# One encoder block on one core: high-part and low-part matmuls in turn, with the low part 64 bytes further on

## The chip, the cores and the metric

The kernel runs on one core of one Trainium2 chip. The metric is device time in microseconds (us) for one execution. Every weight and activation is float32. A product in full float32 precision is put together from float32r products: each operand is split into a high part (the value rounded to float32r) and a low part (the remainder), and high x high, high x low and low x high are added up.

## The reference

One layer of an encoder on 256 tokens of width 2048, cut here to what the change touches and what stands around it:

```python
h = _rmsnorm(x, norm1_g)
proj = h @ w_in                       # q, k, v and u: 1536 + 512 + 512 + 512 columns
a = _rmsnorm(_window_attention(q, k, v, sink), attn_out_g)
f = _rmsnorm(_fourier_mix(u, w_fourier), fourier_out_g)
x = x + jnp.concatenate([a, f], axis=-1) @ w_out
up = _rmsnorm(x, norm2_g) @ w_up      # gate and value: 2 x 5504 columns
gate = depthwise_conv(up[..., :D_FF], dw_w) + dw_b
x = x + (gelu(gate) * up[..., D_FF:]) @ w_down
return _rmsnorm(x, normf_g)
```

## The kernel before, in words

The work is cut into units of one weight tile each, 128 partitions x 2048 float32 (1 MB). SP loads a tile into one of three `raw` buffers (`load`, L145). `split` (L158) then makes the two parts: ScalarE rounds the tile into a `hi` tile (L165), VectorE subtracts that from the tile and writes a `lo` tile (L166). There are three `hi` and three `lo` buffers. `split` for unit n + 2 is issued behind the matmuls of unit n (`step`, L327; `ff_step`, L967), so the parts are made while earlier units multiply. ScalarE, VectorE, GpSimd and SP each work through their own list in the order written in the program; no scheduler moves anything.

Two kinds of units matter here.

- *Moving weights* (`moving_weights`, L293; `by_parts`, L1041): a 128 x 128 block of the activation is loaded into TensorE as the stationary operand, and 512 columns of weights stream past it. These are the u and v columns of `w_in`, `w_out`, and the down-projection, which for most of its rows is written as products P1, N3, N4, N5, P2, P6, P7. Each stationary block is loaded for a single matmul.
- *Still weights* (`still_weights`, L305): a 128 x 128 block of weights is loaded as the stationary operand and the activation streams past it. These are q and k (16 units) and gate and value (86 units): 102 units. One unit is 16 blocks k. For the high part of block k all 512 columns of `hk(k)` stream, that is the activation's own high part (columns 0 to 255) and low part (256 to 511). For the low part of block k only the 256 columns of the activation's high part stream. So a unit is 16 matmuls of 512 columns (L315, "hi") and 16 of 256 columns (L315, "lo"), all into one PSUM bank, whose two halves are added up later (L827 to L830).

The order within a still-weights unit, before: first the high parts, except for the last `rest` of them, then all 16 low parts, then the `rest` high parts. `rest` is 0, 1 or 2; for q and k it comes from the list `QK_REST` (L53), for gate and value from a rule that counts the high parts between two runs of low parts modulo 3 (L1108 to L1111). The first two gate and value units are interleaved, 12 blocks each and then 4 blocks each (L1114 to L1125).

Before each matmul TensorE loads that matmul's stationary block. This load runs beside the matmul ahead of it, so while one matmul streams its activation, the next matmul's weights are read from SBUF.

Where the tiles lie is fixed by the program. The activation `hT` (and `hU`, which takes its place for gate and value) starts at byte 34,912 of each partition, which is 96 modulo 128; all its blocks are 2048 bytes apart. The `hi` and `lo` buffers start at bytes 92,960 and 119,072 and are 8704 bytes apart, all 32 modulo 128; a tile may begin `SHIFT` = 16 elements (64 bytes) into its buffer (L151 to L156, with a pair of offsets for each unit in `shifts`, L126 and L135). Before, the u and v units have both parts 64 bytes on (96 modulo 128) and all others have none. If addresses are put into two halves by whether they lie in the first or the second 64 bytes of each 128, then for u and v, for `w_out` (whose activation tiles `cat` lie at 32 modulo 128) and for the products (whose operands `op_...` lie at 32 modulo 128), what streams and what is loaded begin in the same half. In the still-weights units before they begin in opposite halves, for the high and the low parts alike. In the attention scores (L619) the 256 columns that stream and the blocks that are loaded are in the same half.

After the first gate and value tiles, the feed-forward part runs gate and value units in a fixed order (`ff_items`, L70): 16 of them at the start, then units and products in turn (four rounds of `PATTERN`, L67, with 56 products in all), then the rest. The last part of the kernel is four tiles of the down-projection, the final norm and the stores.

Of the kernel before, what the change touches and what calls it, by code (L numbers as in the profile page):

```python
# [13 lines left out]
P = 128  # L14
D = 2048
S = 256
NK = D // P
# [13 lines left out]

U_HEAD, U_ROW = 16, 768

SHIFT = 16

V_G2, V_GA, V_GF, V_DW, V_DB, V_SINK = 0, 16, 28, 32, 161, 204
# [12 lines left out]
QK_ORDER = []  # L49
for _g in range(NKV):  # L50
    QK_ORDER += [("k", _g)] + [("q", _g * GQA + _i) for _i in range(GQA)]

QK_REST = [2, 2, 2, 2, 1, 1, 2, 0, 0, 0, 1, 0, 0, 0, 1, 0]  # L53
N_U, N_V, N_QK = 0, 4, 8
N_OUT = N_QK + len(QK_ORDER)

# [13 lines left out]
def ff_items():  # L70


    def ups(tiles):
        return [(kind, j) for j in tiles for kind in ("gate", "val")]

    items = ups(range(8))
    for g in range(N_GROUPS):
        todo = {
            "u": ups(range(8 * g + 8, 8 * g + 16)),
            "s": [("product", g, c, p) for c in range(2) for p in PRODUCTS[c]],  # L80
        }
        items += [todo[c].pop(0) for c in PATTERN]
        assert not any(todo.values())
    items += [("down", 0, c) for c in range(4)] + ups(LAST)
    items += [("down", 1, c) for c in range(4)] + [("last", c) for c in range(4)]
    return items
# [3 lines left out]
def block_kernel(  # L90
# [18 lines left out]
    nc = tc.nc  # L109
# [10 lines left out]
    def bank(pool, name):  # L120
        return pool.tile([P, 512], F32, tag=pool.name, name=name)
# [1 line left out]

    units = [(w_u_x[i], 2048) for i in range(4)] + [(w_in[i], 2048) for i in range(20)]
    units += [(w_out[i], 2048) for i in range(16)]
    shifts = [(SHIFT, SHIFT)] * 8 + [(0, 0)] * 32  # L126
    n_front = len(units)
    items, up_index = ff_items(), {}
    for n, it in enumerate(items):
        if it[0] == "product":  # L130
            continue
        up_index[n] = len(units)
        if it[0] in ("gate", "val"):
            units.append((w_up[2 * it[1] + (it[0] == "val")], 2048))
            shifts.append((0, 0))  # L135
            continue
        elif it[0] == "down":
            units.append((w_down_late[4 * it[1] + it[2]], 2048))
        else:
            units.append((w_down_last[it[1]], 512 * len(LAST)))  # L140
        shifts.append((0, 0))
    RAW = 3
    raws, halves = {}, {}
# [7 lines left out]
    def parts_of(i):  # L151
        halves[i] = tuple(
            wp.tile([P, 2176], F32R, tag=h, name=f"{h}{i}", bufs=3)[:, s : s + 2048]
            for h, s in zip(("hi", "lo"), shifts[i])
        )
        return halves[i]  # L156
# [44 lines left out]
    def u_part(k, o, n, m=1):  # L201

        rows = ux[k // 4][:, (k < 4) * U_HEAD :].rearrange("p (k c) -> p k c", k=4)
        return rows[:, k % 4 : k % 4 + m, o : o + n]
# [39 lines left out]
    ps = bank(dn, "ps_warm")  # L244
# [57 lines left out]
                ps, ah, wl, start=False, stop=last and q == q0 + len(kk) - 1  # L302
            )

    def still_weights(hi, lo, ps, kk, rest=0):  # L305

        order = [(hi, k) for k in kk[: len(kk) - rest]] + [(lo, k) for k in kk]
        order += [(hi, k) for k in kk[len(kk) - rest :]]
        for n, (w, k) in enumerate(order):
            x = slice(0, S if w is lo else 2 * S)
            nc.tensor.matmul(  # L315
                ps[:, x], w[:, k * P : (k + 1) * P], hk(k)[:, x],
                start=n == 0 and k == 0, stop=k == NK - 1 and n >= len(order) - max(rest, 1),
            )

    def hk(k):  # L320
        return hT[k // 4][:, k % 4, :]
# [18 lines left out]
    def at(when, i, f, *a):  # L340
        when.setdefault(i, []).append((f, a))
# [5 lines left out]
    def unit(i, work):  # L347
        run(before, i)
        work(*halves.pop(i))
        run(beside, i)  # L350
        step(i)
        run(behind, i)
# [6 lines left out]
    for k in range(NK):  # L359
        c, q = k // 4, k % 4  # L360
        if q == 0:
            hi, lo = (t.rearrange("p (k c) -> p k c", k=4) for t in parts_of(c))
        n = 1 if c < 2 else 2
# [3 lines left out]
        if q % n == 0:  # L367
            w, h = u_part(k, 0, FW, n), hi[:, q : q + n, :]
# [3 lines left out]
        if k < 4:  # L372

            for p, w in enumerate([hi, hi, lo]):
                for b in range(2):
# [3 lines left out]
                        start=k == 0 and p == 0, stop=False,  # L379
# [200 lines left out]
    for c in range(4):  # L580

        def work(hi, lo):
            for b in range(2):
                moving_weights(
                    hi, lo, 512, range(4 * c, 4 * c + 4), hk, b, ps_v[b], c == 0, c == 3
                )

        unit(N_V + c, work)
# [139 lines left out]
    for n, (kind, h) in enumerate(QK_ORDER):  # L728

        def work(hi, lo):  # L730
            ps = st["ps", kind, h] = bank(mm, f"ps_{kind}{h}")
            still_weights(hi, lo, ps, range(NK), QK_REST[n])

        unit(N_QK + n, work)

# [21 lines left out]
    def turn_x(c):  # L757
        turn_x_out(c, turn_x_in(c))
# [26 lines left out]
    for n, (c, kq) in enumerate(OUT_ORDER):  # L785
# [15 lines left out]
        if kq >= 2:  # L801
            part = "a" if kq == 2 else "f"
            ps = ps_a[c] if kq < 3 else ps_a[c, "f"]
# [113 lines left out]
    def ring_load():  # L917
        if ring_next[0] < len(ring):
            key = ring[ring_next[0]]
            ring_next[0] += 1  # L920
            ring_tiles[key] = fp.tile([P, 2048], F32, tag="rawd", name="rawd%d%d%s" % key)
            nc.sync.dma_start(ring_tiles[key], weights_of(*key))
# [24 lines left out]
    def first_sums(g, c):  # L947

        a, b = ring_tiles[g, c, "a"], ring_tiles[g, c, "b"]
        x = ring_tiles["x"] = fp.tile([P, 2048], F32, tag="sumw", name=f"sumw{g}{c}", bufs=1)  # L950
        nc.vector.tensor_tensor(x, a, b, ALU.add)
        nc.gpsimd.dma_start(b, weights_of(g, c, "d"), accum_op=ALU.add)
# [14 lines left out]
    def ff_step(n):  # L967
        todo, later[:] = list(later), []
        for f in todo:
            next(f, None)  # L970
        run(beside, n)
        split_item(n + 2)
        for f in todo:
            for _ in f:
                pass
        run(behind, n)
# [64 lines left out]
    def by_parts(ps, o, hi, lo, first, last):  # L1041

        for p in range(4):
            s = slice(p * 512, (p + 1) * 512)
            nc.tensor.matmul(ps, o[:, 0, p, :], hi[:, s], start=first and p == 0, stop=False)  # L1045
            nc.tensor.matmul(ps, o[:, 1, p, :], hi[:, s], start=False, stop=False)  # L1046
            nc.tensor.matmul(ps, o[:, 0, p, :], lo[:, s], start=False, stop=last and p == 3)  # L1047
# [55 lines left out]
        nc.sync.dma_start(out[b * P : (b + 1) * P, k : k + n], y)  # L1103

    rests = {}  # L1108
    for n, it in enumerate(items):
        if it[0] in ("gate", "val"):  # L1110
            rests[n] = (rests[n - 1] + NK) % 3 if n > 2 and n - 1 in rests else 0  # L1111


    pair = []  # L1114
    for q in range(2):
        kind, j = items[q]
        ps = bank(mm, f"ps_{kind}{j}")
        pair.append((ps, *halves.pop(n_front + q)))
        still_weights(*pair[q][1:], ps, range(12), 2)
        if q == 0:  # L1120
            ff_step(0)
            turn_x(3)
            hT[:] = hT2
    for q, (ps, hi, lo) in enumerate(pair):
        still_weights(hi, lo, ps, range(12, NK), q)  # L1125
    tot2 = base.tile([P, 2], F32, tag="tot2", name="tot2")
    nc.vector.tensor_reduce(tot2, ssq2, mybir.AxisListType.X, ALU.add)
    spread(rstd_of(tot2, D, "2"), r2b, "2")
# [4 lines left out]
    for n, it in enumerate(items):  # L1133
        if n < 2:
            continue
        if it[0] == "last":
            break
        if n in (8, 9):
            ring_load()
        if n == 13:  # L1140
            pending.append(lambda: first_sums(0, 0))
        if it[0] in ("gate", "val"):
            kind, j = it
            ps = bank(mm, f"ps_{kind}{j}")
            still_weights(*halves.pop(up_index[n]), ps, range(NK), rests[n])
            ff_step(n)
            up_posts(n, kind, j, ps)
            continue
        if it[0] == "product":
            kind, g, c, p = it  # L1150
            end = g == N_GROUPS - 1
            if (c, p) in held:
                by_parts(held[c, p], parts[p], *halves.pop(it), g == 0, end)
            else:
                ps = bank(mm, f"ps_{p}{g}{c}")
                by_parts(ps, parts[p], *halves.pop(it), True, True)
                at(beside, n + 1, product_out, g, c, p, ps)
            if end and p == "N4":
                for q in range(3):
                    at(behind, n + 1 + q, shared_out, c, q)  # L1160
        else:
            kind, g, c = it
            hi, lo = halves.pop(up_index[n])
            ps = [bank(mm, f"ps_l{g}{c}{b}") for b in range(2)]
            for b in range(2):
                moving_weights(hi, lo, 512, LATE[g], act.get, b, ps[b], True, True)
            at(beside, n + 1, down_out, c, ps)
            if (g, c) == (0, 0):
                gfb = fp.tile([P, D], F32, tag="sumw", name="gfb", bufs=1)
                nc.gpsimd.dma_start(gfb, normf_g.partition_broadcast(P))  # L1170
        ff_step(n)
# [153 lines left out]
```

## Time and profile before

| | |
|---|---|
| Time, median of 3 runs | 954.75 us (954.56 to 954.78) |
| The profiled execution's own time | 954.88 us |
| Its span, first to last instruction | 953.1 us |
| TensorE busy | 943.5 us, 99%, 5085 matmuls |
| VectorE busy | 750.7 us, 79% |
| ScalarE busy | 534.3 us, 56% |
| Gate and value, hi: 1376 matmuls of 512 columns | mean 392 ns each |
| Gate and value, lo: 1376 matmuls of 256 columns | mean 276 ns each |
| Split of a tile, ScalarE (L165) and VectorE (L166) | 133 times each, mean 1903 and 2276 ns |

Matmuls are pipelined: the next one starts long before the one ahead has drained, so the 392 ns of one matmul are no measure of what it costs. What it costs is the distance from its start to the start of the next, called a *step* here. In a timeline row of sixteen matmuls, sixteen steps lie between its start and the start of the row behind it. The chain of waits writes the steps of one line together: a row of it has its start, its length, and the number of matmuls.

### The profile page before, as it was taken

Reading aid. Unit: us, or ns where it says so; the run is one execution under the profiler, and the core shown is the slowest. Engines: PE = TensorE matmul, PEld = TensorE weight load, DVE = VectorE, ACT = ScalarE, POOL = GpSimd, SP = SyncE. Lnnn points to the kernel's source line nnn. Section 1 sums busy time; section 2 is a strip of 40 time slices with the busy share of each in tenths; the row PEclk is TensorE's granted clock in tenths of the full one; section 3 lists DMA queues with packets and bytes.
Section 4 is the critical chain, followed back from the end, with each engine's and each line's share of the span. In section 5 each row is a group of like instructions: output and inputs, shape, how many; then the busy total and the mean of one; then the engine's idle time right before and its main releaser. Section 6 shows DMA issues by size and latency. Waiting matters only on the chain.

```text
span 953.1 us, 12779 instructions
## 1 busy us (share of the span) xinstructions
PE 943.5 (99%) x5085; PEld 813.4 (85%) x5085; DVE 750.7 (79%) x935; ACT 534.3 (56%) x646; POOL 43.4 (5%) x58
## 2 busy tenths in 40 slices
PE   9999999999999999999999999999999999999996
PEld 7888998888888888888888888888888888888885
DVE  7758877566576689787898978988779979888775
ACT  7656766454454446556565555655556755553442
POOL 0000000000000000000000000000000000000003
PEclk9999999999999999999999999999999999999999
DMA  9844444446456676977778787886987697776532
GB/s 367 335 181 147 162 144 166 148 165 218 177 177 236 250 221 194 291 234 259 231 252 248 238 303 225 265 247 216 289 251 242 208 296 219 220 241 219 178 133 89
DMA packets 32108, 211.58 MB, mean 222 GB/s; under 512 B 3504, under 2 KB 4016, under 8 KB 7984
## 3 DMA queue, kind: packets, MB, share of 16 engines
q1 hardware_dynamic: 28448, 184.55, 52.3%
q0 software_dynamic: 3600, 26.22, 14.6%
q8 instruction: 40, 0.66, 0.3%
q14 instruction: 20, 0.16, 0.0%
HBM read 208.65 MB, written 2.10 MB: 221 GB/s over the span
## 4 chain that ended last, share of the span: by engine, by line
PE 98%; DVE 1%; DMA 0%; issue 0%; ACT 0%; POOL 0%; POOLq 0%; DVEq 0%; ACTq 0%
PE ps_gate L315 25%; PE ps_val L315 25%; PE ps_q L315 7%; PE ps_P L1045 3%; PE ps_P L1046 3%; PE ps_P L1047 3%; PE ps_N L1046 2%; PE ps_N L1045 2%; PE ps_k L315 2%; PE ps_a L299 2%; PE ps_a L301 2%; PE ps_N L1047 2%; PE ps_a L300 2%; PE ps_l L301 2%; PE ps_l L300 2%; PE ps_l L299 2%
## 5 line engine op out<-in xcount | busy, mean ns | idle before, releaser
L166 DVE TENSOR_TENSOR lo<-raw,hi 128x2048 fp32r<-128x2048 f32 (+1 forms) x133 | 302.6, 2276 | 54.4 <-ACT hi L165 54.4
L165 ACT ACTIVATE hi<-raw 128x2048 fp32r<-128x2048 f32 (+1 forms) x133 | 253.2, 1903 | 59.6 <-PE ps_l L300 24.9
L315 PE MATMUL ps_gate<-hU,hi 128*128 128x512 f32 x688 | 167.2, 392 | 0.0
L315 PE MATMUL ps_val<-hU,hi 128*128 128x512 f32 x688 | 167.2, 392 | 0.0
L315 PEld LDWEIGHTS ps_gate<-hU,hi 128*128 128x128 f32 x688 | 128.2, 188 | 27.1
L315 PEld LDWEIGHTS ps_val<-hU,hi 128*128 128x128 f32 x688 | 128.2, 188 | 27.1
L315 PEld LDWEIGHTS ps_gate<-hU,lo 128*128 128x128 f32 x688 | 84.6, 188 | 3.8
L315 PEld LDWEIGHTS ps_val<-hU,lo 128*128 128x128 f32 x688 | 84.6, 188 | 3.8
L827 ACT ACTIVATE ft_g<-ps_gate 128x256 f32<-128x256 f32 x43 | 16.5, 384 | 123.0 <-PE ps_gate L315 123.0
L315 PE MATMUL ps_val<-hU,lo 128*128 128x256 f32 x688 | 85.2, 276 | 0.0
L315 PE MATMUL ps_gate<-hU,lo 128*128 128x256 f32 x688 | 85.2, 276 | 0.0
L827 ACT ACTIVATE ft_v<-ps_val 128x256 f32<-128x256 f32 x43 | 16.5, 384 | 91.9 <-PE ps_val L315 91.9
L1045 PE MATMUL ps_P<-hi_P,op_P 128*128 128x512 f32 x128 | 50.2, 392 | 0.0
L1046 PE MATMUL ps_P<-hi_P,op_P 128*128 128x512 f32 x128 | 50.1, 392 | 0.0
L1047 PE MATMUL ps_P<-lo_P,op_P 128*128 128x512 f32 x128 | 49.9, 389 | 0.0
L315 PE MATMUL ps_q<-hT,hi 128*128 128x512 f32 x192 | 47.6, 394 | 0.0
L937 DVE TENSOR_TENSOR lo_N<-sumw,hi_N 128x2048 fp32r<-128x2048 f32 x16 | 36.6, 2290 | 10.1 <-ACT hi_N L936 10.1
L315 PEld LDWEIGHTS ps_q<-hT,hi 128*128 128x128 f32 x192 | 34.9, 188 | 6.5
L829 DVE TENSOR_TENSOR fa_g<-ps_gate,ft_g 128x256 f32<-128x256 f32 x43 | 18.2, 422 | 26.0 <-ACT ft_g L827 25.9
L299 PE MATMUL ps_a<-hi,cat 128*128 128x512 f32 x96 | 37.9, 395 | 0.0
L1046 PE MATMUL ps_N<-hi_N,op_N 128*128 128x512 f32 x96 | 37.6, 392 | 0.0
L1045 PE MATMUL ps_N<-hi_N,op_N 128*128 128x512 f32 x96 | 37.6, 392 | 0.0
(332 smaller groups left out, 1562.1 us busy)
## 6 DMA issues: line engine op xcount, KB each, us to landing
raw<-in_w_up SPq DMA_DIRECT2D x86, 1024.0 KB, 5.4
raw<-in_w_in SPq DMA_DIRECT2D x20, 1024.0 KB, 4.9
raw<-in_w_out SPq DMA_DIRECT2D x16, 1024.0 KB, 4.7
sumw<-in_w_down POOLq DMA_DIRECT2D x16, 1024.0 KB, 8.7
raw<-in_w_down_late SPq DMA_DIRECT2D x8, 1024.0 KB, 4.8
raw<-in_w_down_last SPq DMA_DIRECT2D x4, 768.0 KB, 4.2
ux<-in_w_u_x SPq DMA_DIRECT2D x3, 768.0 KB, 9.3
xs<-in_x SPq DMA_DIRECT2D x4, 512.0 KB, 16.2
```

Source lines behind the costliest of these rows:

```text
L165: nc.scalar.activation(hi[:, 0:n], raw[:, 0:n], AF.Copy)
L166: nc.vector.tensor_tensor(lo[:, 0:n], raw[:, 0:n], f32(hi[:, 0:n]), ALU.subtract)
L299: nc.tensor.matmul(ps, ah, wh, start=first and q == q0, stop=False)
L300: nc.tensor.matmul(ps, al, wh, start=False, stop=False)
L301: nc.tensor.matmul(ps, ah, wl, start=False, stop=last and q == q0 + len(kk) - 1)
L315: nc.tensor.matmul(ps[:, x], w[:, k * P : (k + 1) * P], hk(k)[:, x], start=n == 0 and k == 0, stop=k == NK - 1 and n >= len(order) - max(r ...
L827: nc.scalar.activation(tmp, ps[:, S : 2 * S], AF.Copy)
L829: nc.vector.tensor_tensor(add, ps[:, 0:S], tmp, ALU.add)
L937: nc.vector.tensor_tensor(lo, src, f32(hi), ALU.subtract)
L1045: nc.tensor.matmul(ps, o[:, 0, p, :], hi[:, s], start=first and p == 0, stop=False)
L1046: nc.tensor.matmul(ps, o[:, 1, p, :], hi[:, s], start=False, stop=False)
L1047: nc.tensor.matmul(ps, o[:, 0, p, :], lo[:, s], start=False, stop=last and p == 3)
```

## The change

Within a still-weights unit the high part of block k and the low part of block k now follow one another, k = 0 to 15. The lists that steer `rest` are gone. In the tiles of q, k, gate and value the high part stays at the start of its buffer, and the low part starts 64 bytes further on, so at 96 modulo 128, in the same half as the activation. Nothing else is changed: same matmuls, same sizes, same loads. On ScalarE, VectorE, GpSimd and SP the same instructions stand in the same order as before.

```diff
-QK_REST = [2, 2, 2, 2, 1, 1, 2, 0, 0, 0, 1, 0, 0, 0, 1, 0]
...
-    shifts = [(SHIFT, SHIFT)] * 8 + [(0, 0)] * 32
+    shifts = [(SHIFT, SHIFT)] * 8 + [(0, SHIFT)] * 16 + [(0, 0)] * 16
...
             units.append((w_up[2 * it[1] + (it[0] == "val")], 2048))
-            shifts.append((0, 0))
+            shifts.append((0, SHIFT))
...
-    def still_weights(hi, lo, ps, kk, rest=0):
-        order = [(hi, k) for k in kk[: len(kk) - rest]] + [(lo, k) for k in kk]
-        order += [(hi, k) for k in kk[len(kk) - rest :]]
-        for n, (w, k) in enumerate(order):
-            x = slice(0, S if w is lo else 2 * S)
+    def still_weights(hi, lo, ps, kk):
+        for k in kk:
+            s = slice(k * P, (k + 1) * P)
+            nc.tensor.matmul(ps, hi[:, s], hk(k), start=k == 0, stop=False)
             nc.tensor.matmul(
-                ps[:, x], w[:, k * P : (k + 1) * P], hk(k)[:, x],
-                start=n == 0 and k == 0, stop=k == NK - 1 and n >= len(order) - max(rest, 1),
+                ps[:, 0:S], lo[:, s], hk(k)[:, 0:S], start=False, stop=k == NK - 1
             )
...
-            still_weights(hi, lo, ps, range(NK), QK_REST[n])
+            still_weights(hi, lo, ps, range(NK))
...
-    rests = {}
-    for n, it in enumerate(items):
-        if it[0] in ("gate", "val"):
-            rests[n] = (rests[n - 1] + NK) % 3 if n > 2 and n - 1 in rests else 0
...
-        still_weights(*pair[q][1:], ps, range(12), 2)
+        still_weights(*pair[q][1:], ps, range(12))
...
-    for q, (ps, hi, lo) in enumerate(pair):
-        still_weights(hi, lo, ps, range(12, NK), q)
+    for ps, hi, lo in pair:
+        still_weights(hi, lo, ps, range(12, NK))
...
-            still_weights(*halves.pop(up_index[n]), ps, range(NK), rests[n])
+            still_weights(*halves.pop(up_index[n]), ps, range(NK))
```

## The prediction

> **What bounds the kernel now.** I read the page's busy shares first, then its slices, then the chain of waits by line.
>
> ```profile
> span 953.1 us, 12779 instructions
> PE 943.5 (99%) x5085; PEld 813.4 (85%) x5085; DVE 750.7 (79%) x935; ACT 534.3 (56%) x646; POOL 43.4 (5%) x58
> PEclk9999999999999999999999999999999999999999
> PE 98%; DVE 1%; DMA 0%; issue 0%; ACT 0%; POOL 0%; POOLq 0%; DVEq 0%; ACTq 0%
> PE ps_gate L315 25%; PE ps_val L315 25%; PE ps_q L315 7%; PE ps_P L1045 3%; PE ps_P L1046 3%; PE ps_P L1047 3%; PE ps_N L1046 2%; PE ps_N L1045 2%; PE ps_k L315 2%; PE ps_a L299 2%; PE ps_a L301 2%; PE ps_N L1047 2%; PE ps_a L300 2%; PE ps_l L301 2%; PE ps_l L300 2%; PE ps_l L299 2%
> ```
>
> TensorE is the whole path: 98% of the chain, at a granted clock that never falls. The still-weights units (L315: gate, val, q, k) are 59% of it. Nothing else needs to be made faster or can be; what counts is the step from one matmul to the next, times 1632 matmuls of 512 columns and as many of 256. Busy shares cannot show this, since a matmul's own length (392 ns) overlaps the next. So I took steps from the chain, where a row has a unit's length, and from the timeline, where sixteen matmuls stand in a row.
>
> Chain, in the stretch where gate and value units follow each other with nothing between, and timeline of the same place:
>
> ```profile
> 302.69 5.48 PE ps_gate L315 x32
> 308.17 5.47 PE ps_val L315 x32
> ...
> 319.11 5.48 PE ps_val L315 x32
> 324.59 5.47 PE ps_gate L315 x32
> 330.06 2.06 PE ps_val L315 x9
> ```
>
> ```profile
> 302.07 0.62 PE L315 MATMUL ps_val<-hU,hi 128*128 128x512 f32 x2
> 302.52 3.83 PE L315 MATMUL ps_gate<-hU,hi 128*128 128x512 f32 x16
> 306.19 1.98 PE L315 MATMUL ps_gate<-hU,lo 128*128 128x256 f32 x16
> 308.00 3.60 PE L315 MATMUL ps_val<-hU,hi 128*128 128x512 f32 x15
> ```
>
> Five units take 330.06 - 302.69 = 27.37 us, 5.474 each. Inside one, 16 hi steps take 306.19 - 302.52 = 3.67 us (229.4 ns each) and 16 lo steps 308.00 - 306.19 = 1.81 us (113.1 ns each). A hi/lo pair costs 342.2 ns.
>
> Are these floors? The 512-column matmuls of u and v say no for hi, and eight units say that lo can be worse:
>
> ```profile
> 23.90 0.23 PE ps_u L301
> ...
> 30.93 0.23 PE ps_v L299
> ```
>
> ```profile
> 59.98 0.44 PE ps_y L527 x4
> 60.42 5.57 PE ps_q L315 x32
> ```
>
> ```profile
> 60.17 3.46 PE L315 MATMUL ps_q<-hT,hi 128*128 128x512 f32 x14
> 63.48 2.05 PE L315 MATMUL ps_q<-hT,lo 128*128 128x256 f32 x16
> 65.36 0.63 PE L315 MATMUL ps_q<-hT,hi 128*128 128x512 f32 x2
> ```
>
> Between the first pair of rows lie 31 steps in 7.03 us: 226.8 ns each, with the same 512 columns and the same load of 128. In the last three rows, the 16 lo steps take 65.36 - 63.48 = 1.88 us, 117.5 ns each: same shape, same addresses modulo 128 as the 113.1 ns ones. So a step is not set by its shape alone. It depends on where the streamed and the loaded block lie towards each other (u and v begin in the same half of 128 bytes, gate in opposite halves), and on the moment at which a run is entered: the good lo run stands behind 2 + 16 = 18 high parts, a multiple of 3, the bad one behind 14 that follow other work. A run keeps the state in which it was entered.
>
> One more row shows lo with both in the same half: the attention scores.
>
> ```profile
> 85.42 0.72 PE ps_s L619 x6
> ```
>
> Six steps of 256 columns take 0.72 us, 120 ns each. That gives a table of four: 512 columns, same half 226.8, opposite 229.4; 256 columns, same half 120, opposite 113.1 once settled well, 117.5 otherwise.
>
> **The change part by part.** *What streams beside what.* While hi block k streams, lo block k is now loaded, which the 64 bytes put into the activation's half: the 226.8 ns cell. While lo block k streams, hi block k + 1 is loaded, in the opposite half: the 113.1 ns cell. The pair becomes 226.8 + 113.1 = 339.9, I take 340 ns and 5.44 us a unit. Against 5.474 that is 34 ns a unit, times 102 units: -3.5 us. Nothing covers it and it covers nothing: all of it is on the path.
>
> *The eight badly entered units.* Six among q and k, and the first two full units of gate and value, stand in the chain with 5.55 to 5.67 us (q at 60.42 above is one):
>
> ```profile
> 79.44 5.55 PE ps_k L315 x32
> ...
> 93.18 5.67 PE ps_q L315 x32
> ...
> 269.66 5.56 PE ps_gate L315 x32
> 275.21 5.57 PE ps_val L315 x32
> ```
>
> Their lo runs cost (117.5 - 113.1) x 16 = 70 ns more: 8 x 0.070 = -0.6 us if all lo steps are in the good state.
>
> *The joins.* No row shows 512 and 256 columns in turn; before, there are two changes of kind in a unit, afterwards 31. From below: the unit of 3.67 + 1.81 = 5.48 us leaves nothing for its two joins, so a join can be free, and a step's cost belongs to its own pair. From above: each step keeps knocking the other out of its good state, hi at 229.4 and lo at 117.5, 346.9 ns a pair. I take the free join, since u and v hold 226.8 ns through changes of both operands and lo holds 113.1 in all but eight units.
>
> *Entering a unit.* Behind a product or behind small matmuls the first steps of a unit are longer until it settles:
>
> ```profile
> 491.98 5.50 PE ps_val L315 x32
> 497.48 0.23 PE ps_P L1045
> 497.71 0.24 PE ps_P L1046
> ...
> 500.22 5.50 PE ps_gate L315 x32
> ```
>
> 5.50 against 5.474 is 26 ns for each entry, and the product pays some too: 12 steps in 500.22 - 497.48 = 2.74 us, 20 ns over 12 x 226.8. By the order of the program a unit is entered in this way about 66 times (55 behind products, 11 behind small matmuls). Afterwards the entry may cost nothing, as products and hi steps now have the same relation of halves, or a unit may never settle, 16 x 6.9 = 110 ns. I take 36 ns, ten more than now, because every second step on the way is a lo step that costs when it is unsettled: +0.7 us. Products are entered from a lo step before and after: no difference.
>
> *Weight loads.* Their number stays. The shortest step must cover one: the row of four ps_y matmuls above, of some 128 columns each, steps in 0.44 / 4 = 110 ns with a load in each, so a load fits into 113. Each lo step already covers one.
>
> *The low part is wanted sooner.* The first lo matmul is now the second of its unit and no longer the fifteenth to seventeenth, some 3 us earlier. What stands ready, at the tightest place that I found:
>
> ```profile
> 749.53 2.29 DVE L166 TENSOR_TENSOR lo<-raw,hi 128x2048 fp32r<-128x2048 f32 x1
> 752.73 3.61 PE L315 MATMUL ps_gate<-hU,hi 128*128 128x512 f32 x15
> ```
>
> The subtraction ends at 751.82, 0.91 us ahead of the unit's first matmul. So no wait. Were this cover gone, TensorE would stand at the second matmul, and behind it all matmuls, then ScalarE's copy of that bank (L827). The tiles' 64 bytes cost the writer nothing: L166 has a median of 2292 ns where the offset is already in use, and the same where it is not:
>
> ```profile
> L166 DVE TENSOR_TENSOR lo<-raw,hi x5: 2285/2292/2293, 24.4 to 44.1; 128x2048 fp32r<-128x2048 f32 x5
> L166 DVE TENSOR_TENSOR lo<-raw,hi x11: 2287/2292/2295, 299.5 to 359.8; 128x2048 fp32r<-128x2048 f32 x11
> ```
>
> *The high part is let go later*, at the unit's end and no longer 1.81 us ahead of it. Its buffer's next writer is a split on ScalarE behind a copy that waits for that unit's end anyway:
>
> ```profile
> 505.76 0.38 ACT L827 ACTIVATE ft_g<-ps_gate 128x256 f32<-128x256 f32 x1 [3.73 <-PE ps_gate L315]
> 506.04 1.91 ACT L936 ACTIVATE hi_N<-rawd10d 128x2048 fp32r<-128x2048 f32 x1
> ```
>
> So nothing. No DMA and no instruction of another queue is moved.
>
> *Sum:* -3.5 - 0.6 + 0.7 = -3.4 us. The profiled execution took 954.88, 0.13 over the median of 954.75, so 951.48 for its like and 951.4 us for the median.
>
> **The rivals.** *The two kinds do not fit each other (slower).* A bad lo run stays bad through sixteen steps, so it does not heal itself; if a hi step of 226.8 needs another entry moment than a lo step of 113.1, alternating leaves every pair at 346.9 ns. A unit then takes 5.55 us: 102 x (5.55 - 5.474) - 0.6 = +7.2, 962 us. It decides from a mean pair of 343.4 ns upwards (342.2 plus 1.9 us over 1632 pairs). For it speaks that high parts before were counted by threes to hit a good moment, so moments matter; against it, that both good states repeat step after step without drift.
>
> *Only units entered behind products stay unsettled.* 55 x (5.55 - 5.50) = +2.8, the other 47 gain 47 x 0.034 = 1.6 and 0.6: +0.6, 955.3 us. For it: entries there are all alike, so what happens once happens 55 times.
>
> *The order and the offset do nothing.* Sixteen steps of each kind add up to 5.474 us in any order: 954.75 us. Against it stand 113.1 beside 117.5 and 226.8 beside 229.4 in rows of the same shapes. The Trainium skill (TensorE: Matmul & The Clock Gate, Step-by-step: what each phase is for) says that TensorE has two independent read ports, and that loading the next tile's weights does not steal read bandwidth from the running matmul. By that rule this rival would be right; the trace disagrees with it by 2.6 ns in a hi step and 4.4 ns in a lo step.
>
> *The entry heals at once:* then 66 x 26 ns go as well: -3.5 - 0.6 - 1.7 = -5.8, 949.0 us.
>
> **How the numbers follow.** 0.2%, 1.9 us, is about what a measurement of this kernel can tell from no change. Forecast 0.58 (949.9 to 952.8), entry healed 0.06, units behind products unsettled 0.10, no effect 0.09, slower 0.17. Faster 0.64, same 0.19, slower 0.17. The forecast's own range is 949.9 to 952.8 by entries of 10 to 60 ns. The range that should hold 8 in 10 goes up through the two cases of no change into the slower one, where only some units stay unsettled: 949.8 to 957.6.
>
> **What would show it.** In the chain, unbroken gate and value units at 5.44 us and those behind products at 5.45 to 5.48. No q, k, gate or value unit over 5.60 but those that begin behind a wait. VectorE's and ScalarE's lists in the same order, TensorE without idle time before a unit's second matmul. Wrong: a unit of 5.50 or more in the unbroken stretch (joins cost), 5.474 there (no effect), or good unbroken units and 5.55 behind products (entries do not settle).

## The result, and the profile after

| | before | after |
|---|---|---|
| Time, median | 954.84 us (954.56 to 955.54, 7 runs) | 951.62 us (951.33 to 952.11, 7 runs) |
| Ratio to before | | 0.9966, 95% interval 0.9954 to 0.9977 |
| The profiled execution's own time | 954.88 us | 951.68 us |
| Its span | 953.1 us | 949.9 us |

The change saves 0.34%. The page's first lines after:

```profile
span 949.9 us, 12779 instructions
PE 940.3 (99%) x5085; PEld 813.4 (86%) x5085; DVE 750.6 (79%) x935; ACT 534.5 (56%) x646; POOL 43.4 (5%) x58
```

The same instructions, and TensorE busy for 3.2 us less. Next the chain of waits after, where two gate and value units follow each other with nothing between. High and low parts are on two lines now (L308 and L309), so a row is one step and no longer a unit; the rows shown are each unit's first:

```profile
302.23 0.23 PE ps_gate L308
...
307.67 0.23 PE ps_val L308
...
313.11 0.23 PE ps_gate L308
```

A unit takes 5.44 us (307.67 - 302.23, and 313.11 - 307.67), 340 ns for each of its sixteen pairs, where it took 5.474. The timeline shows both kinds of step inside it:

```profile
305.12 0.39 PE L308 MATMUL ps_gate<-hU,hi 128*128 128x512 f32 x1
305.35 0.28 PE L309 MATMUL ps_gate<-hU,lo 128*128 128x256 f32 x1
305.46 0.39 PE L308 MATMUL ps_gate<-hU,hi 128*128 128x512 f32 x1
```

From hi to lo 0.23, from lo to hi 0.11: both at their good step. Where the 3.2 us came from is read off the places where the stages begin. From the timelines, the first row of each stage, before and then after:

```profile
54.23 2.10 PE L315 MATMUL ps_k<-hT,hi 128*128 128x512 f32 x8
...
162.51 0.40 PE L299 MATMUL ps_a<-hi,cat 128*128 128x512 f32 x1
...
257.18 2.01 PE L315 MATMUL ps_gate<-hU,hi 128*128 128x512 f32 x8
...
362.76 0.39 PE L1045 MATMUL ps_P<-hi_P,op_P 128*128 128x512 f32 x1
...
851.61 0.39 PE L299 MATMUL ps_l<-hi,act 128*128 128x512 f32 x1
```

```profile
54.13 0.48 PE L308 MATMUL ps_k<-hT,hi 128*128 128x512 f32 x1
...
162.49 0.40 PE L298 MATMUL ps_a<-hi,cat 128*128 128x512 f32 x1
...
257.15 0.39 PE L308 MATMUL ps_gate<-hU,hi 128*128 128x512 f32 x1
...
361.90 0.39 PE L1038 MATMUL ps_P<-hi_P,op_P 128*128 128x512 f32 x1
...
848.65 0.39 PE L298 MATMUL ps_l<-hi,act 128*128 128x512 f32 x1
```

| Stage | before | after | difference |
|---|---|---|---|
| q and k (54.23 to 162.51) | 108.28 | 108.36 | +0.08 |
| `w_out` (to 257.18) | 94.67 | 94.66 | -0.01 |
| first gate and value units (to 362.76) | 105.58 | 104.75 | -0.83 |
| units and products in turn (to 851.61) | 488.85 | 486.75 | -2.10 |

The last stretch, with six more gate and value units, gives 0.2, and q and k begin 0.10 us earlier behind a stretch that the change does not touch. So gate and value gave all of the gain and q and k nothing, though their sixteen units were changed in the same way. The reason is in the chain after, in the attention part:

```profile
65.89 0.44 PE ps_y L520 x4
66.34 0.23 PE ps_q L308
...
71.24 0.23 PE ps_q L308
71.47 0.12 PE ps_q L309
71.59 0.23 PE ps_q L308
71.82 0.12 PE ps_q L309
71.94 0.71 PE ps_s L612 x6
```

This q unit has 71.94 - 66.34 = 5.60 us. Its last two hi steps start 71.59 - 71.24 = 0.35 us apart, not 0.34: at the end of the unit it still has not settled. Seven of the sixteen q and k units are like it ("stuck" from here on), and stay at 350 ns a pair from first to last; the other nine reach 340.

### The profile page after: what moved, and what is told of

It reads as the page before. It is cut to its first block, busy times and chain, and to the rows that moved or that the text cites. A ratio compares the mean times of both kernels' runs of the same rounds, so it can differ in the third digit from the quotient of the medians.

```text
span 949.9 us, 12779 instructions
## 1 busy us (share of the span) xinstructions
PE 940.3 (99%) x5085; PEld 813.4 (86%) x5085; DVE 750.6 (79%) x935; ACT 534.5 (56%) x646; POOL 43.4 (5%) x58
## 4 chain that ended last, share of the span: by engine, by line
PE 98%; DVE 1%; DMA 0%; issue 0%; ACT 0%; POOL 0%; POOLq 0%; DVEq 0%; ACTq 0%
PE ps_gate L308 16%; PE ps_val L308 16%; PE ps_gate L309 8%; PE ps_val L309 8%; PE ps_q L308 5%; PE ps_P L1039 3%; PE ps_P L1038 3%; PE ps_P L1040 3%; PE ps_q L309 2%; PE ps_N L1039 2%; PE ps_N L1038 2%; PE ps_a L300 2%; PE ps_a L298 2%; PE ps_N L1040 2%; PE ps_a L299 2%; PE ps_k L308 2%
## 5 line engine op out<-in xcount | busy, mean ns | idle before, releaser
L308 PE MATMUL ps_gate<-hU,hi 128*128 128x512 f32 x688 | 236.8, 389 | 0.0
L308 PE MATMUL ps_val<-hU,hi 128*128 128x512 f32 x688 | 236.8, 389 | 0.0
L309 PE MATMUL ps_gate<-hU,lo 128*128 128x256 f32 x688 | 190.2, 276 | 0.0
L309 PE MATMUL ps_val<-hU,lo 128*128 128x256 f32 x688 | 190.2, 276 | 0.0
L308 PEld LDWEIGHTS ps_gate<-hU,hi 128*128 128x128 f32 x688 | 129.1, 188 | 27.1
L308 PEld LDWEIGHTS ps_val<-hU,hi 128*128 128x128 f32 x688 | 129.1, 188 | 27.1
L309 PEld LDWEIGHTS ps_gate<-hU,lo 128*128 128x128 f32 x688 | 129.1, 188 | 1.1
L309 PEld LDWEIGHTS ps_val<-hU,lo 128*128 128x128 f32 x688 | 129.1, 188 | 1.1
L820 ACT ACTIVATE ft_g<-ps_gate 128x256 f32<-128x256 f32 x43 | 16.5, 384 | 121.1 <-PE ps_gate L309 121.1
L820 ACT ACTIVATE ft_v<-ps_val 128x256 f32<-128x256 f32 x43 | 16.5, 385 | 89.9 <-PE ps_val L309 89.9
L308 PE MATMUL ps_q<-hT,hi 128*128 128x512 f32 x192 | 66.9, 393 | 0.0
L309 PE MATMUL ps_q<-hT,lo 128*128 128x256 f32 x192 | 53.2, 277 | 0.0
L308 PEld LDWEIGHTS ps_q<-hT,hi 128*128 128x128 f32 x192 | 36.1, 188 | 7.2
L1039 PE MATMUL ps_N<-hi_N,op_N 128*128 128x512 f32 x96 | 37.6, 392 | 0.0
```

Of the source, the lines that this page charges most:

```text
L308: nc.tensor.matmul(ps, hi[:, s], hk(k), start=k == 0, stop=False)
L309: nc.tensor.matmul(ps[:, 0:S], lo[:, s], hk(k)[:, 0:S], start=False, stop=k == NK - 1)
L820: nc.scalar.activation(tmp, ps[:, S : 2 * S], AF.Copy)
```

## The experiments

The theory on trial: what a step costs is decided by where the streamed block and the loaded block lie, not by the order as such. A load is called *good* here when it lies as the prediction's table wants it: in the half of its stream for 512 columns, in the opposite half for 256. The rivals were the order alone, the offset alone, and any offset.

**The order without the offset, and the offset without the order.** First the order alone:

```diff
-    shifts = [(SHIFT, SHIFT)] * 8 + [(0, SHIFT)] * 16 + [(0, 0)] * 16
+    shifts = [(SHIFT, SHIFT)] * 8 + [(0, 0)] * 16 + [(0, 0)] * 16
...
-            shifts.append((0, SHIFT))
+            shifts.append((0, 0))
```

> High and low parts in turn, without the 64 bytes (both kinds load from the half opposite to the streamed activation). Theory (a step is set by its length and by the halves of what streams and what is loaded beside it): hi steps lose their gain, 229 ns or more, and lo steps, entered from hi steps at shifting moments, cost 113 to 118 ns; a pair of 342 to 347 ns, 955 to 962 us, I expect 960. Rival (the order alone brought the gain): 951.6 us, as the changed kernel. Rival (neither matters): 954.8.

Measured 966.05 us, ratio 1.0123 (1.0106 to 1.0139). Then before's order with the low part 64 bytes on:

```diff
-    shifts = [(SHIFT, SHIFT)] * 8 + [(0, 0)] * 32
+    shifts = [(SHIFT, SHIFT)] * 8 + [(0, SHIFT)] * 16 + [(0, 0)] * 16
...
-            shifts.append((0, 0))
+            shifts.append((0, SHIFT))
```

> The order of before (runs of high parts, runs of low parts, with its rests), and the low part 64 bytes further on. Theory: in the low run both now begin in the same half, the 120 ns cell of the table; hi stays at 229; a pair of 349 ns, 1632 x 7 ns = 11 us slower than before, 966 us. Rival (the offset alone brought the gain): 951.6 us. Rival (neither matters): 954.8.

Measured 964.86 us, ratio 1.0103 (1.0086 to 1.0120). Each half of the change alone makes the kernel 10 to 11 us slower; together they make it 3 us faster. The chain of the order alone, first hi step of two units in a row, and that of the offset alone, whole units:

```profile
311.29 0.24 PE ps_val L308
...
316.95 0.23 PE ps_gate L308
```

```profile
310.15 5.58 PE ps_val L315 x32
315.73 5.57 PE ps_gate L315 x32
```

5.66 us and 5.58 us a unit. The sign was as expected in both; the order alone is worse than my worst pair of 347 ns, at 5.66 / 16 = 354. And the theory does not cover it: with the order alone every load lies towards its stream as it did before, 64 bytes off in both kinds of step, and the kernel is 11 us slower. With that relation the order counts by itself. Before, a run of high parts went in threes of 226, 229 and 232 ns (the trace has starts in whole ns) and a run of low parts held 113; in turn, hi steps have 230 to 236 and lo steps 118 to 124.

**Both parts further on, and the wrong one further on**, both with high and low parts in turn. `shifts` has `(SHIFT, SHIFT)` for q, k, gate and value in the one, `(SHIFT, 0)` in the other.

> High and low parts in turn, both 64 bytes further on, so everything begins in the same half. Theory: hi 226.8 ns, lo in the bad cell at 120 ns or more: a pair of 347 ns, 962 us. Rival (the same half is good for both kinds): 951 us or less.

Measured 963.13 us, ratio 1.0088 (1.0071 to 1.0104).

> High and low parts in turn with the offset on the high part instead of the low part: every load in the wrong cell (hi steps load from the opposite half, lo steps from the same). Theory: the worst of the four: 229 to 232 and 120, a pair of 350 ns or more, 966 us or more. Rival (any 64 bytes between the two parts will do): 951.6 us.

Measured 964.44 us, ratio 1.0102 (1.0086 to 1.0117): not the worst, but among the slow ones. Of the four ways to put none, one or both parts 64 bytes on, with parts in turn, only the one of the change is fast.

**Is it the taking of turns?** If only places count, runs of high parts and runs of low parts should do as well, with the offset on the high part, so that hi loads hi from the same half and lo loads lo from the opposite one.

```diff
-    shifts = [(SHIFT, SHIFT)] * 8 + [(0, 0)] * 32
+    shifts = [(SHIFT, SHIFT)] * 8 + [(SHIFT, 0)] * 16 + [(0, 0)] * 16
...
-            still_weights(hi, lo, ps, range(NK), QK_REST[n])
+            still_weights(hi, lo, ps, range(NK), 0)
...
-            still_weights(*halves.pop(up_index[n]), ps, range(NK), rests[n])
+            still_weights(*halves.pop(up_index[n]), ps, range(NK), 0)
```

> All high parts, then all low parts, with the HIGH part 64 bytes further on and the low part not: within a run hi loads from the same half, lo from the opposite one, so both good cells without any turn-taking. Theory (halves alone): 226.8 and 113.1 within the runs, 340 ns a pair; two joins a unit lie in the wrong cell and may each cost 3 to 40 ns: 951.5 to 955 us. Rival (turn-taking itself is needed): hi steps stay at 229, 954.8 us or more.

Measured 961.29 us, ratio 1.0067 (1.0052 to 1.0082). The expectation missed. Its timeline:

```profile
309.08 3.85 PE L315 MATMUL ps_val<-hU,hi 128*128 128x512 f32 x16
312.77 2.05 PE L315 MATMUL ps_val<-hU,lo 128*128 128x256 f32 x16
314.65 3.62 PE L315 MATMUL ps_gate<-hU,hi 128*128 128x512 f32 x15
```

The lo run takes 314.65 - 312.77 = 1.88 us, 117.5 ns a step: the bad lo run that eight units showed before. And 16 hi steps take 312.77 - 309.08 = 3.69, no better than before: in the trace they begin at 241 ns and reach 227 only in their last five. In each unit two steps load from the wrong place: the last hi step loads low block 0, the last lo step loads the next unit's high block 0. A new theory follows: one wrong load at a join is enough to spoil the run behind it. It can be tested by repairing the joins alone. In the next kernel, the same runs stand in the same order, but block 0 of each part lies in the other half; only `split` and the slices know of it:

```diff
+            for h, l, r, m in ((0, 16, 0, 128), (144, 160, 128, 1920)):
+                nc.scalar.activation(hi[:, h : h + m], raw[:, r : r + m], AF.Copy)
+                nc.vector.tensor_tensor(
+                    lo[:, l : l + m], raw[:, r : r + m], f32(hi[:, h : h + m]), ALU.subtract
+                )
...
+    def block(low, w, k):
+        o = k * P + (SHIFT if low != (k > 0) else 2 * SHIFT if low else 0)
+        return w[:, o : o + P]
```

> All high parts, then all low parts, as in the run before with the high part further on, but the first block of each part lies in the other half: high block 0 without an offset, high blocks 1 to 15 64 bytes on, low block 0 64 bytes on, low blocks 1 to 15 128 bytes on. So every single load, at the two joins of a unit too, lies in the good cell of the table. The split needs two instructions on each engine. Theory (the cells decide, and a join in the wrong cell spoilt the earlier run): unbroken gate and value units of 5.44 us without any turn-taking, no lo run at 118; behind products the walk of ten steps that the v columns show, some 42 ns; 951.5 to 953.5 us. Rival (it is the turn-taking that keeps the steps in their good state): lo runs at 118 or hi steps at 229 again, 958 us or more.

Measured 951.04 us, ratio 0.9961 (0.9948 to 0.9975): the time of the change, without taking turns. Chain and timeline:

```profile
312.86 5.44 PE ps_gate L334 x32
318.30 5.44 PE ps_val L334 x32
```

```profile
307.26 3.79 PE L334 MATMUL ps_val<-hU,hi 128*128 128x512 f32 x16
310.88 1.98 PE L334 MATMUL ps_val<-hU,lo 128*128 128x256 f32 x16
312.70 3.79 PE L334 MATMUL ps_gate<-hU,hi 128*128 128x512 f32 x16
```

16 hi steps in 3.62 us (226.3 each), 16 lo steps in 1.82 (113.8). Modulo 128, thirty of a unit's thirty-two loads lie towards their stream as in the run before (the low blocks behind the first have moved by a whole 128 bytes); the two at the joins do not, and 10 us went. Modulo 256 these low blocks went from 64 bytes below their stream to 64 above it. That alone does not explain the gain, since the low parts of before, also 64 below, had runs of 113 ns. Taking turns is not what makes the step short. It is one way in which every hi step loads a block from the good place and so does every lo step, the joins included.

**The stuck q and k units.** The changed kernel, with q and k in another order from the second block on:

```diff
+        order = [(hi, 0), (lo, 0)] + [(w, k) for k in range(1, NK) for w in (lo, hi)]
...
-            still_weights(hi, lo, ps, range(NK))
+            mixed(hi, lo, ps)
```

> The changed kernel, but in q and k the order is high 0, low 0, low 1, high 1, low 2, high 2 and so on: one low step behind a low step, and another moment from then on. Theory: seven of the sixteen q and k units are stuck in a pair of 350 ns because of the moment at which they are entered; a knock of 5 to 7 ns behind the first pair lets some of them out. If all: 7 x 0.15 = 1 us less, 950.6 us; if the knock catches others instead, no change. Rival (these units are slow because of what VectorE or ScalarE does beside them): the same seven units stay slow.

Measured 951.01 us, ratio 0.9959 (0.9945 to 0.9972). All seven came free. In its chain the k unit that begins behind six score matmuls at 78.53, in the place of a stuck one, is over when the next transposes (`ps_t`) begin:

```profile
78.53 0.71 PE ps_s L622 x6
...
84.72 0.44 PE ps_t L672 x4
```

84.72 - 78.53 - 0.71 = 5.48 us for it, where it had 84.88 - 78.57 - 0.71 = 5.60 in the changed kernel:

```profile
78.57 0.71 PE ps_s L612 x6
...
84.88 0.44 PE ps_t L662 x4
```

So it was not the work beside them on VectorE and ScalarE that kept these units slow, for that work is the same. In the trace of the changed kernel the stuck units behind score matmuls begin with a hi step of 230 ns, the free ones with 226 or 227. With the swapped order the same three begin with 230 again, and reach 340 a pair behind the displaced low step. One displaced step lets a unit out; that it gets stuck through the moment at which it is entered fits this, but no run varied the moment alone.

**How large must the offset be?** The changed kernel with the low part 128 bytes further on (`2 * SHIFT`), and later 192 (`3 * SHIFT`).

> The changed kernel with the low part 128 bytes further on instead of 64. Theory (the half of 128 bytes decides): the same as the order alone without an offset, 966 us. Rival (any distance between the parts will do): 951.6 us.

Measured 961.01 us, ratio 1.0061 (1.0046 to 1.0076). The distance matters, but this is not the 966 us of no offset, which is the same half of 128 bytes. By my theory the two are one case, so halves of 128 bytes are not the rule.

**Into the products.** Between a unit and a product what streams changes from activation to weights. A product still pays for that, and the unit behind it again. If that is the same matter, it can be laid out too. On top of the run with the first block in the other half: product weights 64 bytes on, all operand blocks but the first used 64 bytes on, and that one used once; high block 0 further on in units behind a product.

```diff
-        o = fp.tile([P, 2, 4, P], F32R, tag=f"op_{name}", name=f"op_{name}", bufs=1)
+        o = fp.tile([P, 1056], F32R, tag=f"op_{name}", name=f"op_{name}", bufs=1)
+        high = o[:, 144:656].rearrange("p (k c) -> p k c", k=4)
+        low = o[:, 656:1040].rearrange("p (k c) -> p k c", k=3)
...
-            nc.tensor.matmul(ps, o[:, 0, p, :], hi[:, s], start=first and p == 0, stop=False)
-            nc.tensor.matmul(ps, o[:, 1, p, :], hi[:, s], start=False, stop=False)
+            nc.tensor.matmul(ps, o[1][p], hi[:, s], start=first and p == 0, stop=False)
+            nc.tensor.matmul(ps, o[0][p], hi[:, s], start=False, stop=False)
```

To make room, the weight buffers were cut from 2176 to 2080 elements.

> The run with the first block in the other half, carried on to the products: their weights stream from 64 bytes further on, all their operand blocks but the first used lie 64 bytes further on, the first is used once, and in units behind a product high block 0 lies 64 bytes on too. So each load within units, products and their joins lies in the good cell. Theory (the cells and the moment of entry explain the walks at both ends of a product): products of 2.72 us, all gate and value units at 5.44 us; 55 x 15 ns and 56 x 25 ns go, 2.2 us: 948.9 us against 951.1 of that run. Rival (the walks are the price of changing from still to moving weights, whatever the addresses): no change, 951 us; VectorE's 56 further instructions might even cost.

Measured 965.42 us, ratio 1.0112 (1.0098 to 1.0126): 16.5 us over what was expected. The changed kernel was run beside it:

> The changed kernel itself, so that the run with the products can be compared on the same chip: 951.6 us.

Measured 951.83 us, ratio 0.9972 (0.9961 to 0.9984). The chain of the run with the products shows units at no common length any more:

```profile
402.16 5.61 PE ps_val L342 x32
...
410.53 5.54 PE ps_gate L342 x32
...
418.87 5.52 PE ps_val L342 x32
```

What it has that no kernel before had is buffers of 2080 x 4 = 8320 bytes, 65 x 128. The half of 128 bytes is as planned in each, but from one buffer to the next the place modulo 256 differs by 128. Together with the 128-byte run this suggests that places count modulo 256. So the same once more, with 2112 elements (33 x 256 bytes) and operand tiles of 1088 instead of 1056:

> The run with the products once more, with buffers of a multiple of 256 bytes. In the run before, the weight buffers had been shortened to 8320 bytes, which keeps the half of 128 but puts every second buffer 128 bytes off modulo 256; its steps were at 230 to 241 wherever streamed and loaded block lay 128 apart modulo 256. Theory A (the address modulo 256 decides, equal is good for 512 columns): all good cells again, products of 2.72 us and units of 5.44: 948.9 us. Theory B (the failure came from the changed order or the split instructions): 960 us or more again. Rival C (the walks at the ends of products are the price of the change of kind): 951 us.

Measured 948.85 us (948.11 to 949.22), ratio 0.9933 (0.9921 to 0.9946). And its opposite, the changed kernel with a low part in the right half of 128 bytes but 128 off modulo 256:

> The changed kernel with the low part 192 bytes further on instead of 64: the same half of 128 bytes, but 128 bytes from the activation modulo 256. Theory A (modulo 256 decides): hi steps of 230 to 241 ns, 960 us or more. Theory B (the half of 128 bytes decides, as I had it): 951.6 us.

Measured 961.09 us, ratio 1.0063 (1.0047 to 1.0078). The chains of the two runs:

```profile
396.98 5.44 PE ps_val L342 x32
402.42 0.23 PE ps_P L1079
...
404.91 0.23 PE ps_P L1081
405.14 5.44 PE ps_gate L342 x32
```

```profile
309.17 0.23 PE ps_val L308
...
314.71 0.23 PE ps_gate L308
```

With the products laid out as well, a unit behind a product has 5.44 us like any other, and a product 405.14 - 402.42 = 2.72 us, twelve steps of 226.7: nothing is left to settle. With 192 bytes a unit has 314.71 - 309.17 = 5.54 us. Its total is what I expected for modulo 256, its steps are not: I expected hi steps of 230 to 241, and a pair has only 346 ns. By the starts in its trace, hi steps have 228.3 ns and lo steps 118.3, so the lo steps pay more, though the blocks that they load lie as in the changed kernel. A load that is off in one step spoils the other too.

The buffers of 33 x 256 bytes say one thing more. From one to the next the place differs by 256 bytes, so it changes modulo 512, and 82 of the 84 gate and value units that run in one piece still have 5.44 us. A distance of 256 bytes does no harm here; one of 128 does.

The kernel with the products beats both: 6.3 us faster than before, and 2.8 us faster than the change by the two medians, which were not taken side by side.

## Why the prediction was right

Predicted 951.4 us, measured 951.62. The sum of 3.4 us came out at 3.2 us. The step that carried it was right; that the total came so close is luck, since what was counted for entries and what was counted for q and k were off by 0.6 and about 1 us in opposite directions.

- **The pair, -3.5 us over 102 units.** Right: 5.44 us in the unbroken stretch, from 226.7 and 113.3. The 86 gate and value units got it, some 3 us; q and k did not.
- **Free joins.** Right for this change: 5.44 leaves nothing for thirty-one changes from one kind of step to the other. The step behind it was too general. I took it that a join is free because before's two joins seemed to be; the two runs of high parts and low parts, without and with block 0 in the other half, showed that, with every other load good, a join is free only if its load comes from the good place too. In the change every join's does.
- **Entering a unit, taken at 36 ns.** Too high: units behind products have 5.46 us, 20 ns over 5.44. Chain after:

```profile
498.79 0.23 PE ps_gate L308
...
504.25 0.23 PE ps_N L1038
...
507.00 0.23 PE ps_val L308
```

  That is 504.25 - 498.79 = 5.46 us for the unit, and 2.75 for the product, as before. The 26 ns for before were read from rows rounded to 10 ns; by the starts in the traces an entry cost 20 ns before (5.495 against 5.4755) and 22 after. So an entry costs 2 ns more, not ten, and of the +0.7 us some 0.6 were too much. (By 66 entries the forecast's own range would also be 949.7 to 953.0; nothing hangs on it.)
- **The eight badly entered units, -0.6 us.** Six of the eight did come good, four of q and k and both of gate and value, each by 0.10 to 0.13 us. What failed is the step from there to all 102 units, that every unit settles. I took every lo step to be in its good state, and left 110 ns an entry as a bound only. Seven q and k units took the unsettled course for their whole length: two of the eight, and five that were well entered before. Such a unit pays 10 ns a pair, 160 ns. Here is one of the five, before and then after:

```profile
107.63 5.48 PE ps_k L315 x32
```

```profile
106.56 0.72 PE ps_s L612 x6
...
112.88 0.44 PE ps_t L662 x4
```

  It had 5.48 us and has 112.88 - 106.56 - 0.72 = 5.60. So q and k lost 0.08 us, where I had counted on a gain of about 1 us. The rival in which some units never settle was true, but of units behind small matmuls and not of those behind products, where I had looked for it.
- **The low part, wanted sooner.** No wait: the tightest subtraction that I had found ends at 749.31 us after the change, 1.10 us ahead of the unit's first lo matmul at 750.41, and the trace shows no idle time of TensorE in the gate and value units.

The rule of the Trainium skill by which loading the next weights takes nothing from the running matmul (TensorE: Matmul & The Clock Gate, Step-by-step: what each phase is for) would have given 954.8 us for every kernel here that only moves addresses or puts the same matmuls in another order. They go from 951.0 to 966 us, so the measurement decides against it here.

The two rivals with the whole gain on one side fell: neither the order nor the offset does anything good alone.

## What to carry to other kernels

Where TensorE is the bound and each stationary block is used once, measure start to start, not busy time, and try where streamed and loaded blocks lie towards each other modulo 256 bytes, for each length of stream by itself. Lay out the joins between kinds of work with the same care as the runs: here two wrong loads in thirty-two cost 10 us of 951. Check that a padded buffer keeps its place modulo 256 from one copy to the next, and look for units that never settle behind small matmuls.

## What the runs showed of the hardware

With weights of 128 x 128 float32r loaded beside the stream, the runs in which every step is settled take 226.7 ns for 512 columns when the loaded block lies at the same place as the streamed one modulo 256 bytes, and 113.3 ns for 256 columns when it lies 64 bytes below or above it (below in the changed kernel; above, but for a unit's last lo step, in the run with block 0 in the other half). In the kernels tried in which some loads lie otherwise, gate and value units in the unbroken stretch took 5.53 to 5.66 us instead of 5.44. Before's own relation, 64 bytes below for both kinds, had two prices: 5.474 us in runs counted by threes, 5.66 in turn.

With parts in turn, the mean pair of an unbroken unit was, layout by layout, 340.0, 346.7, 350.0 or 353.3 ns: 3.3 ns or a multiple of it apart. Why, no run shows.

A run of steps keeps a slow course for a whole unit, as the stuck q and k units and the lo runs of 117.5 ns show, and one displaced step can end it. What decides the course at entry is not shown: the engines beside it do not, the moment is argued, and no run measured the mechanism inside the memory or TensorE. Nor is it settled why no offset (966 us) is worse than 128 bytes (961 us). Where the tiles lie is taken from the program's layout; the profiles do not show addresses.
